# A hybrid encoder layer: weights split ahead of the feature tiles, and written orders from the decay terms to the merge

## The chip, the cores and the metric

The kernel runs on one core of a Trainium2 chip. The time is device microseconds of one execution; three executions of the kernel before give the median. A profiled execution has a trace of every instruction beside its time.

## What is computed

One layer, 256 tokens and 16 meta tokens (L = 272 positions) of 2048 features, float32:

```python
u = rmsnorm(h); proj = u @ W_in
# branch A: q, k = silu(conv3(...)); bidirectional mLSTM cell, 4 heads x 256
b = cumsum(log_sigmoid(f))
dmat = b[t] - b[s] + i[s];  m_t = max(...)
s = (q @ k.T) * exp(dmat - m_t)
hs = (s @ v) / maximum(abs(sum(s)), exp(-m_t)); head norm over 256
# branch B: differential attention, 8 heads, partial rotary on q and k
merged = sigmoid(g_A) * (A @ W_A) + sigmoid(g_B) * (B @ W_B)
h += merged @ W_out
h += ConvGLU(RMSNorm(h)); final RMSNorm
```

The forward and the backward cell are each computed in one piece, with the cumulative log decays on the rows of a matrix.

## The kernel before

All matrix products run with features or tokens on the 128 partitions. Every float32 operand is split into a high half (`hi`, a cast on ScalarE, line 157) and a low half (`lo`, a subtraction on VectorE, line 115), and `product` (line 172) issues three matmuls for each pair of operands: hi by hi, hi by lo, lo by hi. The weights come in pieces of 4 x 128 rows by 256 columns (512 KB), in the order of the list `pieces`. SyncE loads them (line 200) into six buffers, `prepare` splits them into four pairs of buffers, and `gemm` runs 24 matmuls on each piece. `gemm` is a generator: it yields after each piece, and `weave` steps a second generator once for each piece, so that the cell's work lies between pieces. What stands in the list `later` is issued at the next `flush`, after a piece.

The stages that matter here, in order:

- The opening: the tokens' features are turned (transposed on TensorE, line 349), scaled and split, two at a time, and the first block of query weights (pieces 0 to 3) is multiplied as the features come (`gq`, k = 0 to 15). Behind it are 32 small matmuls for the cell's gates (`gg`, the rows with 32 output columns), and the norm of the tokens, spread over the partitions by `spread_norm`. This whole stage stands inside `in_order()`: each engine runs it in the order in which it is written.
- The queries (pieces 4 to 15) and keys (16 to 31), with `conv_silu` behind each block: a multiplication by the norm that evacuates the accumulator, three taps of a convolution, Silu, split. Beside them `decay_terms` turns the gates into the decays. There are three accumulators `acc`, two per block, so that the second accumulator of a block needs the evacuation of the first of the block before.
- The values (32 to 47), transposed and centred by `turn`; beside them `heads1`: for each head the decays (a broadcast on GpSimd and exponentials), the scores, and the sums of the scores.
- The feature queries of branch B (`roped(dq)`, 48 to 63); beside them `heads2`: the reciprocal of the sums, `spread`, `merged`, `outputs`, `normed`.
- The feature keys (`roped(dk)`) and all that follows, to the end of the span.

Outside of `in_order()` a scheduler with a cost model decides, before the kernel is built, in which order each engine runs its instructions; data dependences bind it, the written order doesn't.

```python
def weave(front, back):
    for _ in front:
        next(back, None)
    run(back)
```

## Time and profile before

| | |
|---|---|
| three runs, us | 1567.14, 1569.33, 1570.07 (median 1569.33) |
| profiled execution, us | 1567.37 |
| its span, us | 1565.5 |
| instructions | 28927 |
| busy: TensorE, VectorE, ScalarE, GpSimd, us | 1542.6, 1028.6, 763.7, 81.0 |

The span runs from the first to the last instruction of the core; 1.9 us of the profiled execution's time lie outside it. An engine is busy while it runs an instruction; matmuls overlap one another, so TensorE's busy time doesn't say at which pace they run. In the rows, an operand's name is that of its tile, PE is TensorE, ACT ScalarE, DVE VectorE, POOL GpSimd, SP SyncE.

### The profile page before, as it was taken

What the parts mean: (1) busy time and instruction counts of PE and PEld (TensorE: products, weight loads), DVE (VectorE), ACT (ScalarE), POOL (GpSimd) and SP (SyncE); (2) the same over time, 40 slices, a digit from 0 to 9 for tenths busy, and PEclk for the clock granted to TensorE, in tenths of its full rate; (3) what the DMA queues carried; (4) which work ended last, traced back from release to release, by engine and by line L of the source; (5) the groups of instructions that cost most, each with busy time, mean ns of one, the idle gap of its engine ahead of it and who ended that gap; (6) DMA issues with size and microseconds to landing.
All of it is one profiled execution on the core that took longest, in us unless ns stands there. A gap on an engine that the chain in (4) does not pass through costs nothing.

```text
span 1565.5 us, 28927 instructions
## 1 busy us (share of the span) xinstructions
PE 1542.6 (99%) x11825; PEld 1491.2 (95%) x11825; DVE 1028.6 (66%) x1617; ACT 763.7 (49%) x1147; POOL 81.0 (5%) x120
## 2 busy tenths in 40 slices
PE   8899989999999999999999999999999999999997
PEld 8899989999999999999999999999888999999887
DVE  6786688758886545665666676666444676766554
ACT  5656445444655433554555444444333444545443
POOL 1130113100000000000110000000000000000000
PEclk9999999999999999999999999999999999999999
DMA  8365425654356655555555556555555556655552
GB/s 261 110 202 161 148 83 166 189 166 132 122 175 202 185 179 188 181 180 185 193 169 181 187 185 187 181 183 180 198 190 188 187 177 188 185 181 185 184 195 95
DMA packets 255386, 274.53 MB, mean 175 GB/s; under 512 B 11492, under 2 KB 233317, under 8 KB 255237
## 3 DMA queue, kind: packets, MB, share of 16 engines
q1 hardware_dynamic: 251378, 268.61, 54.1%
q10 hardware_dynamic: 3875, 4.07, 0.8%
q8 instruction: 93, 1.52, 0.4%
q14 instruction: 40, 0.33, 0.1%
HBM read 270.55 MB, written 2.10 MB: 174 GB/s over the span
## 4 chain that ended last, share of the span: by engine, by line
PE 95%; DVE 2%; ACT 1%; issue 1%; POOL 0%; DMA 0%; SPq 0%; DVEq 0%; POOLq 0%; ACTq 0%
PE acc L172 90%; PE two L172 2%; DVE lo L115 1%; PE two L846 1%; PE one L172 0%; PE one L858 0%; PE two L568 0%; POOL t L712 0%; ACT hi L157 0%; DMA r<-in_norm_g_dram 0%; PE two L977 0%; PE two L965 0%; DVE u L730 0%; DVE u L115 0%; POOL t L164 0%
## 5 line engine op out<-in xcount | busy, mean ns | idle before, releaser
L172 PE MATMUL acc<-u,hi 128*128 128x258 f32 (+1 forms) x6592 | 1201.8, 285 | 4.8 <-DVE r L161 4.8
L172 PEld LDWEIGHTS acc<-u,hi 128*128 128x128 f32 x6592 | 1019.0, 190 | 7.1 <-DVE r L161 5.1
L172 PE MATMUL acc<-u,lo 128*128 128x258 f32 (+1 forms) x3296 | 925.3, 284 | 0.8 <-DVE lo L115 0.8
L115 DVE TENSOR_TENSOR lo<-raw,hi 128x1024 fp32r<-128x1024 f32 (+1 forms) x500 | 616.8, 1234 | 422.1 <-ACT hi L157 420.4
L157 ACT CAST hi<-raw 128x1024 fp32r<-128x1024 f32 (+1 forms) x500 | 523.7, 1048 | 648.1 <-PE acc L172 501.5
L172 PEld LDWEIGHTS acc<-u,lo 128*128 128x128 f32 x3296 | 622.3, 190 | 1.9 <-DVE lo L115 1.2
L172 PE MATMUL acc<-hi,u 128*128 128x512 f32 (+1 forms) x704 | 209.6, 381 | 0.0
L172 PEld LDWEIGHTS acc<-hi,u 128*128 128x128 f32 x704 | 130.7, 190 | 26.3
L172 PE MATMUL acc<-lo,u 128*128 128x512 f32 (+1 forms) x352 | 134.9, 383 | 0.0
L172 PEld LDWEIGHTS acc<-lo,u 128*128 128x128 f32 x352 | 66.2, 188 | 13.6
L161 DVE TENSOR_TENSOR r<-acc,r 128x258 f32<-128x258 f32 x88 | 37.3, 424 | 12.2 <-PE acc L172 12.2
L115 DVE TENSOR_TENSOR u<-r,u 128x256 fp32r<-128x256 f32 (+2 forms) x93 | 37.7, 435 | 4.9 <-ACT u L157 4.4
L1025 ACT ACTIVATE r<-r,fcT 128x256 f32<-128x256 f32 x88 | 39.8, 500 | 0.0
L157 ACT CAST u<-r 128x256 fp32r<-128x256 f32 (+2 forms) x93 | 34.4, 404 | 9.7 <-DVE r L161 7.0
L1026 DVE SCALAR_TENSOR_TENSOR r<-r,fcT,r 128x256 f32<-128x256 f32 x88 | 38.5, 479 | 0.0
L1027 DVE SCALAR_TENSOR_TENSOR r<-r,fcT,r 128x255 f32<-128x255 f32 x88 | 38.4, 478 | 0.0
L151 ACT ACTIVATE r<-r 128x256 f32<-128x256 f32 (+2 forms) x77 | 29.5, 412 | 3.5 <-DVE r L459 3.1
L161 DVE TENSOR_TENSOR r<-r,r 128x256 f32<-128x256 f32 (+1 forms) x57 | 22.1, 420 | 0.1
L161 DVE TENSOR_TENSOR r<-acc,u 128x258 f32<-128x258 f32 x32 | 13.5, 422 | 12.9 <-PE acc L172 12.9
L164 DVE TENSOR_TENSOR u<-acc,u 128x512 f32<-128x512 f32 (+1 forms) x18 | 10.6, 626 | 13.9 <-PE acc L172 13.9
L161 DVE TENSOR_TENSOR r<-acc,rB 128x272 f32<-128x272 f32 (+1 forms) x38 | 16.1, 429 | 4.8 <-PE acc L172 4.7
L151 ACT ACTIVATE t<-two,sm 128x272 f32<-128x272 f32 x32 | 15.3, 482 | 5.5 <-DVE sm L802 5.5
(246 smaller groups left out, 754.6 us busy)
## 6 DMA issues: line engine op xcount, KB each, us to landing
raw<-in_w_up_dram SPq DMA_DIRECT2D x176, 512.0 KB, 3.9
raw<-in_w_in_dram SPq DMA_DIRECT2D x175, 512.0 KB, 3.5
raw<-in_w_down_dram SPq DMA_DIRECT2D x88, 512.0 KB, 3.7
raw<-in_w_out_dram SPq DMA_DIRECT2D x32, 512.0 KB, 3.3
raw<-in_w_branch_m_dram SPq DMA_DIRECT2D x16, 512.0 KB, 3.3
raw<-in_w_branch_d_dram SPq DMA_DIRECT2D x16, 512.0 KB, 3.2
t<-in_x_dram ACTq DMA_DIRECT2D x8, 256.0 KB, 3.4
xc<-in_x_dram SPq DMA_DIRECT2D x3, 512.0 KB, 6.3
```

What stands on the lines that cost most here:

```text
L115: V.tensor_tensor(out=out, in0=src, in1=hi.bitcast(F32), op=ALU.subtract)
L151: a = S.activation(out, in_, func, **kw)
L157: S.copy(hi, src)
L161: eng.tensor_tensor(out=o, in0=a, in1=b, op=ALU.mult)
L164: eng.tensor_tensor(out=o, in0=a, in1=b, op=ALU.add)
L172: PE.matmul(o, p, q, start=first and i == 0, stop=last and i == len(ops) - 1)
L846: PE.matmul(ps[:, i, 0:L], dq[h // 2][p][o:o + 64, h % 2, 2 + P * qt:2 + P * (qt + 1)], dk[h // 2][q][o:o + 64, h % 2, :], start=(p, q) == ...
L1025: S.activation(z, u[:, 2:NT], AF.Copy, scale=fcT[:, 1, f:f + 1])
L1026: V.scalar_tensor_tensor(out=z, in0=u[:, 1:NT - 1], scalar=fcT[:, 0, f:f + 1], in1=z, op0=ALU.mult, op1=ALU.add)
L1027: V.scalar_tensor_tensor(out=z[:, 0:SEQ - 1], in0=u[:, 3:NT], scalar=fcT[:, 2, f:f + 1], in1=z[:, 0:SEQ - 1], op0=ALU.mult, op1=ALU.add)
```

## The change

In the opening, piece i+1 is split ahead of the four groups of features that piece i meets, not after the second; the pieces 4 to 6 are prepared at k = 11, 13 and 15. From the decay terms to the feature keys, three `weave` calls move inside `in_order()`, so that the written order now holds there on every engine. And the written order changes: `conv_silu`'s evacuation only multiplies, and its taps, its Silu with the cast, and its low half each come one piece later (by `later`); `decay_terms` starts three pieces later; `decays` is divided into a broadcast and the exponentials, `scores` into the products, their weighing and their halves, `merged` into the merge and its halves, `outputs` and `normed` into the squares, the variance and the rest; the sums of a head are issued one head later, those of the last head in `heads2`, which is followed by the feature keys in the same `weave`. The absolute value of the sums becomes a maximum of the sums and their negatives on VectorE. `roped` rotates over three pieces. The number of matmuls stays the same.

```diff
         for k in range(16):
             if k % 4 == 0:
                 wq = weights(0)
+                if k < 12:
+                    prepare(k // 4 + 2)
             for ci in range(2):
                 product(gq[:, ci, :L], [([p[:, P * ci:P * (ci + 1)] for p in wq[k % 4]], [p[:, k % 2, :] for p in us[k // 2]])],
                         first=(k == 0), last=(k == 15))
             while turned < min(16, 2 * k + 4, k + 5):
                 turn(turned)
                 turned += 1
-            if k % 4 == 1:
-                prepare(k // 4 + 2)
             if k >= 5 and k % 2:
                 squares((k - 5) // 2)
             if k == 12:
 
                 split(wg[:, :, 0:16], wg[:, :, 16:32], graw)
-            if k in (12, 14):
-                prepare(k // 2)
+            if k in (11, 13, 15):
+                prepare((k - 1) // 2)
...
+        uc = []
+
+        def taps():
+            for ci, (u, c) in enumerate(uc):
+                S.activation(c, u, AF.Copy, scale=cw(1, f + ci))
+            for ci, (u, c) in enumerate(uc):
+                V.scalar_tensor_tensor(out=c[:, 1:nt], in0=u[:, 0:nt - 1], scalar=cw(0, f + ci), in1=c[:, 1:nt],
+                                       op0=ALU.mult, op1=ALU.add)
+                V.scalar_tensor_tensor(out=c[:, 0:nt - 1], in0=u[:, 1:nt], scalar=cw(2, f + ci), in1=c[:, 0:nt - 1],
+                                       op0=ALU.mult, op1=ALU.add)
+            later.append(silu)
+
+        def silu():
+            for ci, (_, c) in enumerate(uc):
+                activation(c, c, AF.Silu)
+                S.copy(hi[:, ci, :], c)
+            later.append(rest)
+
+        def rest():
+            for ci, (_, c) in enumerate(uc):
+                low(lo[:, ci, :], c, hi[:, ci, :])
+
         def evac(ci, a):
-            j = f + ci
-            u, c = r1(nt), r1(nt)
-            mul(u, a, r)
-            S.activation(c, u, AF.Copy, scale=cw(1, j))
-            V.scalar_tensor_tensor(out=c[:, 1:nt], in0=u[:, 0:nt - 1], scalar=cw(0, j), in1=c[:, 1:nt],
-                                   op0=ALU.mult, op1=ALU.add)
-            V.scalar_tensor_tensor(out=c[:, 0:nt - 1], in0=u[:, 1:nt], scalar=cw(2, j), in1=c[:, 0:nt - 1],
-                                   op0=ALU.mult, op1=ALU.add)
-            activation(c, c, AF.Silu)
-            split(hi[:, ci, :], lo[:, ci, :], c)
+            uc.append((r1(nt), r1(nt)))
+            mul(uc[ci][0], a, r)
+            if ci == 1:
+                later.append(taps)
...
     def decay_terms():
+        for _ in range(3):
+            yield
 
         pli, plf = two(), two()
         for d in range(2):
             PE.matmul(pli[:, d, :L], sel[0:32, d * P:(d + 1) * P], gsb[0:32], start=True, stop=True)
             PE.matmul(plf[:, d, :L], sel[0:32, (2 + d) * P:(3 + d) * P], gsb[0:32], start=True, stop=True)
         li, lf, e, y, w = (unit([2, L]) for _ in range(5))
+        yield
         S.copy(lf, plf[:, :, :L])
         S.copy(li, pli[:, :, :L])
...
+    with in_order():
+        weave(decay_terms(), chain(queries(), keys()))
...
+    last = []
+
     def heads1():
         activation(en, m[:, :, T0:L], AF.Exp, scale=-1.0)
-        decays(0)
+
+        broadcast(0)
+        broadcast(1)
         yield
         for h in range(4):
-            if h < 3:
-                decays(h + 1)
-            hl = scores(h)
-            yield
-            yield
-            yield
-            sums(h, hl)
-            yield
+            yield
+            decays(h)
+            yield
+            if h:
+                sums(h - 1, last[-1])
+            sc = scores(h)
+            yield
+            fs = weighed(h, sc)
+            if h < 2:
+                broadcast(h + 2)
+            yield
+            last.append(halved(fs))
 
     vm, gen = values(V0, True)
-    weave(heads1(), gen)
+    with in_order():
+        weave(heads1(), gen)
...
     def heads2():
+
+        yield
+        sums(3, last[3])
+        yield
         rec = unit([2, NT])
-        S.activation(rec, den[:, :, 0:NT], AF.Abs)
-        V.tensor_tensor(out=rec, in0=rec, in1=en, op=ALU.max)
+        V.scalar_tensor_tensor(out=rec, in0=den[:, :, 0:NT], scalar=-1.0, in1=en, op0=ALU.mult, op1=ALU.max)
+        V.tensor_tensor(out=rec, in0=den[:, :, 0:NT], in1=rec, op=ALU.max)
+        yield
         V.reciprocal(rec, rec)
+        yield
         rhl = pair(NT)
         split(*rhl, rec)
         yield
-        hl = merged(0, spread(0, rhl))
-        yield
+        rc = spread(0, rhl)
+        yield
+        FB = merged(0, rc)
+        yield
+        hl = halves(FB)
         yield
         for h in range(4):
+            num = outputs(h, hl)
+            yield
+            hi, lo = squared(num)
             if h < 3:
                 rc = spread(h + 1, rhl)
-            o = outputs(h, hl)
             yield
             if h < 3:
-                hl = merged(h + 1, rc)
-            normed(h, *o)
-            yield
-            yield
-            yield
+                FB = merged(h + 1, rc)
+            yield
+            if h < 3:
+                hl = halves(FB)
+            var, r = variance(hi, lo)
+            yield
+            normed(h, num, var, r)
...
-    weave(heads2(), roped(dq, DQ0, T0, NT))
-    run(roped(dk, DK0, 0, L))
+    with in_order():
+        weave(heads2(), chain(roped(dq, DQ0, T0, NT), roped(dk, DK0, 0, L)))
```

On TensorE, from the last matmul of the opening to the first of the gates. `acc` and `hi_396`, `lo_397` are accumulators and halves of piece 4 before, `two_171` is the gates' sum. Before:

```order
L172 MATMUL two_170<-u_166,lo_357 128x272
L172 MATMUL acc_559<-u_152,hi_396 128x258
L172 MATMUL acc_559<-u_153,hi_396 128x258
L172 MATMUL acc_560<-u_152,hi_396 128x258
L172 MATMUL acc_560<-u_153,hi_396 128x258
L172 MATMUL two_171<-u_152,u_172 32x272
```

In the change, the end of that stretch, where `hi_388` and `lo_389` are the halves of piece 4; ahead of it stand 18 more matmuls of piece 4:

```order
L172 MATMUL acc_532<-u_154,hi_388 128x258
L172 MATMUL acc_532<-u_155,hi_388 128x258
L172 MATMUL acc_532<-u_154,lo_389 128x258
L172 MATMUL acc_532<-u_154,hi_388 128x258
L172 MATMUL acc_532<-u_155,hi_388 128x258
L172 MATMUL two_171<-u_152,u_172 32x272
```

The gates stood behind 4 matmuls of piece 4, all of high halves; now they stand behind 23, with the low half among them.

On VectorE among the queries, up to the evacuation of an accumulator. Before, `r1_839` is that of the first accumulator of the third block of queries, behind the decay terms and their scans:

```order
L502 SCALAR_TENSOR_TENSOR u_548<-u_548,u_549 128x544
L505 SCALAR_TENSOR_TENSOR u_539<-u_548,u_547 128x272
L506 SCALAR_TENSOR_TENSOR u_539<-u_548,u_547 128x272
L512 MEMSET u_768 128x272
L516 SCALAR_TENSOR_TENSOR r1_771<-u_548,u_768 128x272
L525 SCALAR_TENSOR_TENSOR r1_805<-u_548,u_768 128x16
L161 TENSOR_TENSOR r1_839<-acc_703,rB_173 128x258
```

In the change, the evacuation of the second block's first accumulator (`r1_822`), behind three operations of the decay terms (`u_638`, `u_639`, `u_637`) and the low half of piece 13 (`lo_793`):

```order
L516 TENSOR_SCALAR u_638<-u_637 128x544
L517 TENSOR_SCALAR u_639<-u_638 128x544
L518 TENSOR_TENSOR u_637<-u_637,u_639 128x544
L115 TENSOR_TENSOR lo_793<-raw_686,hi_792 128x1024
L161 TENSOR_TENSOR r1_822<-acc_680,rB_173 128x258
L161 TENSOR_TENSOR r1_825<-acc_681,rB_173 128x258
L161 TENSOR_TENSOR u_637<-u_637,u_639 128x544
L115 TENSOR_TENSOR lo_834<-raw_722,hi_833 128x1024
```

On ScalarE in the change, the Abs, Exp, Ln and Exp of the decay terms and the casts of the pieces 12 to 14 (`hi_755`, `hi_792`, `hi_833`):

```order
L513 ACTIVATE u_637<-u_636 128x544
L142 ACT_TABLE_LOAD
L147 ACTIVATE u_637<-u_637 128x544
L157 CAST hi_755<-raw_644 128x1024
L151 ACTIVATE u_638<-u_638 128x544
L151 ACTIVATE u_639<-u_638 128x544
L157 CAST hi_792<-raw_686 128x1024
L157 CAST hi_833<-raw_722 128x1024
```

The scans no longer stand ahead of an evacuation here; a cast of weights now stands behind Ln and Exp, and an evacuation behind the low half that needs this cast.

On VectorE at the end of the values, in the change: the last weighing of scores (`FB_2022`), the reduction and the scaling of the last values, the low half of a piece (`lo_2485`), the low half of the last head's scores (`t2_2425`), and the sums' maximum and reciprocal (`u_2520`):

```order
L667 SCALAR_TENSOR_TENSOR FB_2022<-one_2358,FB_2022 16x2
L598 TENSOR_REDUCE sm3_2477<-two_2470 128x3
L599 TENSOR_SCALAR sm3_2477<-sm3_2477 128x3
L115 TENSOR_TENSOR lo_2485<-raw_2327,hi_2484 128x1024
L115 TENSOR_TENSOR t2_2425<-t2_2417,t2_2424 128x516
L609 SCALAR_TENSOR_TENSOR v0_1586<-two_2470,sm3_2477,v0_1585 16x256
L609 SCALAR_TENSOR_TENSOR u_2234<-two_2470,sm3_2477,u_2233 128x256 x2
L789 SCALAR_TENSOR_TENSOR u_2520<-two_1583,u_1584 128x516
L790 TENSOR_TENSOR u_2520<-two_1583,u_2520 128x516
L115 TENSOR_TENSOR lo_2524<-raw_2381,hi_2523 128x1024
L792 RECIPROCAL u_2520<-u_2520 128x516
```

Before, the low half of the scores stood ahead of the reduction, and the products that take it were spread among the matmuls of the feature queries; in the change TensorE has them behind 24 matmuls of the first piece of the feature queries and six transposes.

## Rows read from the trace of the kernel before

**Rows 1.** The page: the span, and the shares of the chain that ended last.

```profile
span 1565.5 us, 28927 instructions
...
PE 95%; DVE 2%; ACT 1%; issue 1%; POOL 0%; DMA 0%; SPq 0%; DVEq 0%; POOLq 0%; ACTq 0%
```

**Rows 2.** Waits of TensorE: us in total, times, longest.

```profile
PE acc L172 <- DVE r L161: 4.8, 1, 4.8
PE two L172 <- issue: 2.8, 1, 2.8
PE two L172 <- DVE lo L115: 1.8, 3, 0.7
...
PE two L172 <- DVE u L723: 1.0, 1, 1.0
PE acc L172 <- DVE lo L115: 0.8, 2, 0.5
PE one L172 <- POOL t L712: 0.5, 1, 0.5
PE two L172 <- DVE u L115: 0.3, 1, 0.3
```

**Rows 3.** Timeline of the opening: start, us, engine, line, operation, idle before.

```profile
22.63 9.70 SPq L200 DMA_DIRECT2D raw<-in_w_in_dram  x9
...
26.41 1.05 ACT L157 CAST hi<-raw 128x1024 fp32r<-128x1024 f32 x1 [1.35 <-DVE u L115]
...
27.49 1.23 DVE L115 TENSOR_TENSOR lo<-raw,hi 128x1024 fp32r<-128x1024 f32 x1 [1.10 <-ACT hi L157]
...
27.59 0.66 PE L172 MATMUL acc<-u,hi 128*128 128x258 f32 x4
...
28.09 4.14 PE L172 MATMUL two<-u 128*32 128x272 f32 x32
```

**Rows 4.** Busy time by window: PE, PEld, DVE, ACT, POOL, granted clock, DMA.

```profile
68.67:73.10 4.43, 4.43 (x20) 4.43 (x21) 4.43 (x15) 2.63 (x5) 0.00 (x0) 0.50 0.01 4
209.84:213.06 3.22, 3.22 (x17) 3.22 (x16) 3.22 (x12) 1.75 (x2) 0.86 (x1) 0.50 0.00 0
229.50:233.00 3.50, 3.50 (x30) 3.46 (x29) 3.50 (x9) 2.24 (x4) 2.47 (x2) 1.00 0.00 0
```

**Rows 5.** Timeline of the queries.

```profile
47.12 0.86 DVE L457 SCALAR_TENSOR_TENSOR r<-r,prmT,r 128x257 f32<-128x257 f32 x2
...
59.91 0.72 DVE L494 TENSOR_TENSOR u<-u 128x544 f32<-128x544 f32 x1
59.94 0.28 PE L172 MATMUL acc<-u,lo 128*128 128x258 f32 x1
...
60.30 0.28 PE L172 MATMUL acc<-u,lo 128*128 128x258 f32 x1
...
60.72 0.66 ACT L151 ACTIVATE u<-u 128x544 f32<-128x544 f32 x1 [1.02 <-DVE u L494]
...
61.40 1.28 ACT L147 ACT_TABLE_LOAD   x1
...
62.70 0.42 ACT L147 ACTIVATE r<-r 128x258 f32<-128x258 f32 x1
...
69.26 0.42 PE L172 MATMUL acc<-u,lo 128*128 128x258 f32 x1
...
69.91 0.42 PE L172 MATMUL acc<-u,lo 128*128 128x258 f32 x1
```

**Rows 6.** Busy time of the first eight pieces of the keys, columns as in Rows 4.

```profile
76.79:102.00 25.21, 24.43 (x195) 23.97 (x194) 22.82 (x33) 12.76 (x20) 15.96 (x27) 1.00 0.69 210
```

**Rows 7.** Timeline from the values to the first feature weights.

```profile
199.02 0.70 DVE L115 TENSOR_TENSOR t<-t,t 128x516 fp32r<-128x516 f32 x1 [1.44 <-ACT t L157]
...
199.63 0.95 DVE L573 TENSOR_REDUCE sm<-two 128x3 f32<-128x768 f32 x1
...
203.60 3.38 DVE L730 RECIPROCAL u<-u 128x516 f32<-128x516 f32 x1
```

More of the change, by code (lines that the diff above doesn't have):

```diff
@@ L326, in rsqrt, with newton @@
     def rsqrt(r, ss, n, work, bias=eps):
-        a, t = work
         activation(r, ss, AF.Ln, bias=bias, scale=1.0 / n)
         activation(r, r, AF.Exp, scale=-0.5)
+        newton(r, ss, n, work, bias)
+    def newton(r, ss, n, work, bias=eps):
+        a, t = work
         V.tensor_scalar(out=a, in0=ss, scalar1=1.0 / n, scalar2=bias, op0=ALU.mult, op1=ALU.add)
@@ L545, in queries @@
             yield from gemm(w_in, 16, Q0 + 256 * b, 256, us, T0, NT, conv_silu(qs, 2 * b, rQ, NT))
-    weave(decay_terms(), chain(queries(), keys()))
+    with in_order():
+        weave(decay_terms(), chain(queries(), keys()))
     def values(c0, centred):
@@ L569, in turn, with parts @@
                 pvs = pv[:, :, 0:384].rearrange("p c (s x) -> p s c x", s=3)
+                mu = sm(3)
                 if centred:
-                    mu = sm(3)
                     V.tensor_reduce(out=mu, in_=pvs, axis=AX.XY, op=ALU.add)
                     V.tensor_scalar(out=mu, in0=mu, scalar1=-1.0 / 256, scalar2=None, op0=ALU.mult)
+                later.append(lambda: parts(pvs, mu))
+            def parts(pvs, mu):
                 for s in range(3):
@@ L601, in hybrid_layer, with broadcast @@
     PARTS_W = [(F0c, 0, 0, 258), (F1c, 1, 2, 256), (F2c, 2, 130, 128)], [(B2c, 2, 0, 258), (B1c, 1, 0, 130), (B0c, 0, 0, 2)]
-    def decays(h):
+    def broadcast(h):
         FB = rbp.tile([P, WN], F32, tag="rb", name="FB")
@@ L617, in decays @@
         mask(FB[:, B2c + 130:B2c + 258], P, 0, 1)
+    def decays(h):
+        FB = W[h]
         for d, parts in enumerate(PARTS_W):
@@ L623, in scores @@
     def scores(h):
-        FB = W[h]
         ps, p0 = two(), one()
@@ L629, in scores, with weighed @@
             product(sc[s], [([t[:, c, s0:s0 + P] for t in ks[h]], [t[:, c, :] for t in qs[h]]) for c in range(2)])
+        return sc
+    def weighed(h, sc):
+        FB = W[h]
         for parts in PARTS_W:
@@ L643, in scores, with halved @@
         add(r[0:16, 0:2], r[0:16, 0:2], FB[0:16, B0c:B0c + 2], G)
+        return fs
+    def halved(fs):
         hi, lo = t2([2, NT], F32R), t2([2, NT], F32R)
@@ L698, in merged, with halves @@
         add(FB[:, B2c + 130:B2c + 258], FB[:, B2c + 130:B2c + 258], FB[:, F2c:F2c + P])
+        return FB
+    def halves(FB):
         hl = rbs.tile([P, 2, WN], F32R, tag="w", name="hl")
@@ L708, in outputs, with squared @@
                                        [t[:, 258 * s:258 * s + 258] for t in hl]) for s in range(3)])
+        return num
+    def squared(num):
         sq, hi, lo = t2([2, NT]), t2([2, NT], F32R), t2([2, NT], F32R)
@@ L712, in outputs, with variance @@
         G.tensor_tensor(out=lo, in0=sq, in1=hi.bitcast(F32), op=ALU.subtract)
-        return num, hi, lo
-    def normed(h, num, hi, lo):
+        return hi, lo
+    def variance(hi, lo):
         var = one()[:, 0:NT]
@@ L718, in normed @@
         r = r1()
-        rsqrt(r, var, 256, (r1(), r1()))
+        activation(r, var, AF.Ln, bias=eps, scale=1.0 / 256)
+        activation(r, r, AF.Exp, scale=-0.5)
+        return var, r
+    def normed(h, num, var, r):
+        newton(r, var, 256, (r1(), r1()))
         u = unit([2, NT])
@@ L757, in put, with swap, join @@
             dst.append((hi, lo))
+            sw = unit([2, nt])
+            table = lambda i: rope[:, i:i + 1, t0:t0 + nt].to_broadcast([P, 2, nt])
+            def swap():
+                V.stream_shuffle(sw, u, shuffle)
+                mul(sw, sw, table(1), G)
+                mul(u, u, table(0))
+                later.append(join)
+            def join():
+                add(u, u, sw)
+                S.copy(hi, u)
+                later.append(lambda: low(lo, u, hi))
             def evac(ci, a):
@@ L761, in evac @@
                 if ci == 1:
-                    table = lambda i: rope[:, i:i + 1, t0:t0 + nt].to_broadcast([P, 2, nt])
-                    sw = unit([2, nt])
-                    V.stream_shuffle(sw, u, shuffle)
-                    mul(sw, sw, table(1), G)
-                    mul(u, u, table(0))
-                    add(u, u, sw)
-                    split(hi, lo, u)
+                    later.append(swap)
             return evac
```

1 line of the change is left out of this document (added).

## The prediction

> **What bounds the kernel now.** I read the chain of the profiled execution first: 95% of the span is TensorE's own work [rows 1]. So a change of order on the other engines can only give back time in which TensorE waits, or runs slowly because it has waited. Next I read the waits of TensorE [rows 2], placed each on the timeline, and read the granted clock behind it [rows 4]. What can be recovered lies in three stretches:
>
> - Opening, until 27.6 us: three waits for the low halves of pieces 1 to 3, 1.8 us together.
> - Queries and start of the keys: one wait of 4.8 us (an accumulator is not free, because VectorE evacuates it late) and one of 0.5 us. Behind the long one the granted clock is 0.50, the lower level of 1.2 GHz, for 4.43 us [rows 4].
> - Values to the normalisation of the cell's heads: 2.8 and 0.3 us in which the products `spread` wait for the reciprocals, 1.0 us for a normalised head, 0.5 us for squares from GpSimd. Here too a stretch of 3.22 us at 0.50 follows the long wait [rows 4].
>
> The price of such a slow stretch comes from the pitch of the matmuls. From 59.94 to 60.30 three take 0.36 us, 0.12 each; from 69.26 to 69.91 three take 0.65, 0.215 each [rows 5]. A slow stretch therefore loses 1 - 0.12/0.215 = 0.44 of its length: 2.0 us in the queries, 1.4 us behind the values. The wait of 1.0 us had no such sequel: the window right behind it shows 1.00 [rows 4].
>
> So the change can win at most 1.8 + (4.8 + 0.5 + 2.0 = 7.3) + (2.8 + 0.3 + 1.0 + 0.5 + 1.4 = 6.0) = 15.1 us, 1% of the time, if it leaves no wait and makes none. The matmuls stay the same, and everything behind the feature keys keeps its order, so the whole question is what waits the new orders have. I followed the four queues of the changed program by hand with the durations of before.
>
> **Opening.** The split of piece i+1 now stands in front of the turns of its four tiles, and the three waits should go: the opening's matmuls would end at 27.6 - 1.8 = 25.8 us. But piece 4, the first of the next block, is not there yet. SyncE is still issuing small parameter loads and comes to it at 22.63; the cast on ScalarE runs from 26.41 to 27.46 and the low half on VectorE until 28.72 [rows 3]. The change moves none of that. Before, TensorE spent this time on the 32 gate matmuls (28.09, 4.14 us [rows 3]); in the new order these come behind 23 matmuls of piece 4. So TensorE idles from 25.8 to 27.46, runs two matmuls, and idles until 28.72. The remaining 22 matmuls of piece 4 (2.65 us) and the gates (4.0) end at 35.4. Before, the gates ended at 32.07 and 20 matmuls of the piece were left (2.4 us): 34.5. Result: the 1.8 us are won and lost again, and **0.9 us** more. An idle of 2.7 us out of 2.9 lies near the 2.8 + 0.3 that was followed by the lower clock and far from the 1.0 that was not, but two matmuls interrupt it; I charge half of 1.4, **0.7 us**. Bounds: 0 and 1.4.
>
> The Trainium skill (TensorE: Matmul & The Clock Gate, "Part 1: The HAM clock gate") says that an idle TensorE falls back to 1.2 GHz, at a phase that varies from run to run. The rows behind the long waits agree; by that page my half could be all or none in any execution.
>
> **Queries.** The 4.8 us went because VectorE had scheduled the evacuation of the old accumulator behind a long run of decay terms. In the new order the evacuation stands behind fewer, but TensorE's order is fixed too, with nothing to fill a gap. Four waits remain, counted from the end of the small products that spread the norm (time 0), with 0.35 to 0.42 us for an operation on 258 columns and about 0.7 for one on 544 [rows 5]:
>
> - The gate sums wait for the copy of the norm, three multiplications and a bias, 2.1 us, with 1.4 us of matmuls as cover: 0.7 us.
> - Piece 8: its cast stands behind two taps, the table load (1.28 us [rows 5]), two Silu and two casts, ready at 7.0 where TensorE arrives at 7.1; its low half takes 1.23 us more, and only two matmuls do without it: 0.9 us.
> - The next accumulator: its evacuation stands behind two small low halves and the low half of piece 9, and comes at 10.5; TensorE is there at 9.45: 1.1 us.
> - The accumulator after that. ScalarE ends the second Silu's cast at 14.8; then Abs 0.66, table load 1.28, Exp 0.66 (17.4), cast of piece 12 (18.45). VectorE makes the low half of it (19.7), two small low halves (20.4), and the decay terms' 0.44, 0.44 and 0.72 (21.9). ScalarE's Ln and Exp lie across these, to 22.6, and only then comes the cast of piece 13 (23.65), VectorE's low half of it (24.9), and behind that the evacuation (25.3). TensorE arrives at 22.05: 3.25 us. It is 4.8 us made shorter, not removed.
>
> Sum 5.95 us; and the wait of 3.25 lies between 2.8 + 0.3 and 4.8, which both brought the lower clock: 1.4 us by the nearer one. **7.35 against 7.3: nothing.** Bounds: without the lower clock -1.4; with 2.0 instead +0.6; each wait is the difference of two chains of ten to twenty operations, and I allow 2 us each way for their sum.
>
> In the keys' first half VectorE is busy for 22.82 of 25.21 us already [rows 6]; piece 16 would start at about the same time as before, so I charge no wait there. If VectorE falls behind, the evacuations of the keys wait with it (a rival below).
>
> **Values to the heads.** The chain behind the values is now spread over the steps of the feature queries. The reciprocal (3.38 us [rows 7]) gets four steps of 2.9 us as cover between the sums and `spread`, and the 2.8 + 0.3 us go; I find no wait for the 1.0 and the 0.5 either. But the last head's sums come after a single step of cover. Time 0 is the last matmul of the values: VectorE evacuates (0.6), weighs five blocks (2.7); TensorE has 24 matmuls (2.9) and six transposes (3.5) and then stands before the sums. VectorE goes on with the reduction (3.6 to 4.55, 0.95 [rows 7]), a small scaling (4.7), the low half of a weight piece (5.9) and only then the low half that the sums take (0.70 [rows 7]): 6.6. So a wait of **3.1 us**, as long as the 2.8 + 0.3 that it replaces, and by the same row 1.4 us of slow clock: 4.5 against 6.0, **-1.5 us**. Bounds: -2.9 without the clock; 0 if one of the two small waits stays.
>
> **Sum.** 0.9 + 0.7 + 0.05 - 1.5 = +0.15 us against the profiled execution (1567.37 us, of which 1.9 lie around the span). The median of the three runs is 1.96 above that execution, so the forecast is 1567.37 + 0.15 + 1.96 = 1569.5; I say **1569.3 us**, no change. A difference under 0.2% (3.1 us) is about what a measurement of this kernel can't tell from none.
>
> **Rivals.**
>
> - *The long wait in the queries does not appear.* It hangs on VectorE meeting the low half of piece 13 before the evacuation. If ScalarE's Exp and Ln run 3 us earlier against TensorE (every wait ahead of it shifts TensorE, not them), the 3.25 and its 1.4 fall away, and if the sums' wait also stays at the higher clock (-1.4) and the opening too (-0.7), the time is 1569.3 - 4.65 - 2.1 = 1562.6. For it: TensorE's own waits push it back against the chains, which are then less late. Against it: the chain on ScalarE and VectorE takes 10 us from the second Silu with nothing to shorten it. From 3.1 us on it counts as faster. Chance of faster 0.32.
> - *VectorE becomes the bound in the keys.* The place is 76.79 to 102, where 2.4 us of 25.2 are free on VectorE [rows 6]. In the fixed order an operation that waits (for GpSimd, for ScalarE) holds all behind it, weights' low halves included, so that idle can't be used by others. If VectorE waits 5 us in this stretch, 2.6 more than it has, TensorE loses these 2.6, and at the lower clock 1.4 more: 1569.3 + 4 = 1573.3. It decides from 5.5 us of such waits on. For it: the four waits above are of exactly this kind. Against it: half the decay terms' work was spread evenly over these steps. Chance 0.17.
> - *Every wait of about 1 us drops the clock.* Four such waits (0.7, 0.9, 1.1, and the opening's) at 1.4 each, 5.6 us: 1574.9. The 1.0 us wait with a clock of 1.00 behind it [rows 4] speaks against it. Chance 0.06. [...]
> - *The change does nothing it says*, because the waits merely move: that is my forecast. Chance 0.45.
>
> Faster 0.32, within 0.2% 0.45, slower 0.23. The range reaches from the first rival to the edge of the second and third: 1562 to 1574.5 us.
>
> **What would show it.** In the profile of the changed kernel: no waits of `two` for low halves before 25 us, but an idle of 2.5 to 3 us at 25.8 to 28.7; among TensorE's waits one for VectorE's multiplication (L161) of about 3 us near 64 and one of about 1; one near 205 of about 3 us that ends with VectorE's low half; a granted clock of 0.50 behind the two long ones. The forecast is wrong if one of the 3-us waits is missing (faster), or if waits of TensorE between 77 and 187 us, where there was one of 0.5, add up to over 3 us (slower).

## Result and profile after

The changed kernel takes 1582.59 us, the median of four runs (1578.87 to 1585.48), against 1569.24 of the kernel before on the same chip: ratio 1.0092, 95% interval 1.0079 to 1.0105. It is slower by 0.9%, 8 us past the upper end of the range. The profiled execution, the fastest of the four, took 1578.87 us; the rows below are from it. I read in the same order as before. First the page: the span, and the chain that ended last [rows 1].

```profile
span 1576.2 us, 28904 instructions
...
PE 93%; DVE 3%; ACT 1%; issue 1%; DMA 1%; SPq 0%; POOL 0%; ACTq 0%; DVEq 0%; POOLq 0%
```

The span is 10.7 us longer, and VectorE's share of the chain went from 2 to 3%. Next, what TensorE waited for (us in total, times, longest), to be held against [rows 2]:

```profile
PE two L172 <- DVE u L609: 5.3, 2, 2.7
PE acc L172 <- DVE r L161: 3.4, 2, 2.7
PE acc L172 <- DVE lo L115: 2.8, 4, 1.1
PE two L172 <- DVE t L115: 2.5, 2, 2.2
PE two L172 <- ACT t L157: 1.3, 2, 0.8
PE two L172 <- ACT hi L157: 1.2, 1, 1.2
```

The 4.8 us for an accumulator became 2.7, and the 2.8 for `spread` are gone. But the largest entry is new: 5.3 us for L609, a copy of centred values out of `two`. The rows of these waits on TensorE's timeline, from the opening to the feature keys:

```profile
12.02 0.36 PE L172 MATMUL two<-u,hi 128*128 128x272 f32 x1 [0.82 <-ACT u L354]
13.30 0.37 PE L172 MATMUL two<-u,hi 128*128 128x272 f32 x1 [0.92 <-DVE u L355]
...
29.11 0.39 PE L172 MATMUL acc<-u,lo 128*128 128x258 f32 x1 [0.76 <-DVE lo L115]
...
43.66 0.72 PE L504 MATMUL two<-r,t 32*128 32x272 f32 x2 [0.86 <-ACT r L491]
49.05 0.51 PE L172 MATMUL acc<-u,hi 128*128 128x258 f32 x2 [0.23 <-ACT hi L157]
50.31 0.39 PE L172 MATMUL acc<-u,lo 128*128 128x258 f32 x1 [0.75 <-DVE lo L115]
52.45 0.50 PE L172 MATMUL acc<-u,hi 128*128 128x258 f32 x2 [0.68 <-DVE r L161]
...
66.93 0.51 PE L172 MATMUL acc<-u,hi 128*128 128x258 f32 x2 [2.71 <-DVE r L161]
...
190.34 1.88 PE L172 MATMUL two<-u 128*128 128x258 f32 x12 [2.66 <-DVE u L609]
...
200.48 0.38 PE L172 MATMUL two<-t,selr 128*128 128x258 f32 x1 [0.42 <-ACT t L157]
...
203.06 0.63 PE L172 MATMUL two<-t,selr 128*128 128x258 f32 x3 [2.20 <-DVE t L115]
...
308.99 0.39 PE L172 MATMUL acc<-u,lo 128*128 128x272 f32 x1 [1.09 <-DVE lo L115]
```

Busy time by window, columns as in [rows 4]; the granted clock is the third figure from the end:

```profile
60.00:67.00 7.00, 4.29 (x37) 4.08 (x35) 5.12 (x9) 3.35 (x6) 0.00 (x0) 1.00 0.25 75
67.00:75.00 8.00, 8.00 (x67) 8.00 (x68) 7.27 (x11) 6.71 (x11) 0.00 (x0) 1.00 0.58 176
160.00:170.00 10.00, 6.47 (x48) 5.85 (x47) 3.47 (x7) 3.24 (x7) 1.68 (x4) 1.00 0.28 81
170.00:180.00 10.00, 9.70 (x67) 9.73 (x68) 5.92 (x12) 5.05 (x11) 3.64 (x7) 0.83 0.44 130
190.00:200.00 10.00, 9.66 (x66) 9.53 (x66) 6.01 (x12) 6.32 (x13) 1.69 (x4) 0.83 0.55 170
200.00:210.00 10.00, 7.39 (x59) 7.12 (x59) 8.74 (x11) 3.83 (x6) 0.00 (x0) 1.00 0.30 91
```

Behind the wait of 2.7 us at 66.9 and that of 2.2 us at 203 the clock stays at 1.00; two windows of the values' stage have 0.83, about a third of them at the lower level.

The matmuls are the same in number and nearly in order, so the start of the k-th one tells where the 10.7 us arose. The changed kernel is 1.4 us behind at the 200th (piece 4 and the gates), 0.8 ahead at the 1000th (early in the values), 5.8 behind at the 1800th (where the feature queries end), 7.6 at the 2400th (in the feature keys), 7.7 at the 6400th, 10.65 at the last. So: opening +1.4; queries, keys and the first values -2.2; **values to the heads +6.6**; feature keys +1.8; and about +3 in the feed-forward, where every engine's order is that of before. Of the 6.6, 4.5 are TensorE's waits (9.2 us between the 1000th and the 1800th matmul, against 4.6 before); most of the rest is the second of the two stretches at the lower clock, where before there was one.

**The values' stage, followed back.** TensorE, VectorE and ScalarE around the first long wait, from the timeline:

```profile
163.98 0.88 POOL L164 TENSOR_TENSOR t<-t,FB 16x258 f32<-16x258 f32 x2
164.90 0.62 ACT L157 CAST t<-t 128x516 fp32r<-128x516 f32 x1 [6.84 <-POOL t L164]
165.42 1.04 ACT L157 CAST hi<-raw 128x1024 fp32r<-128x1024 f32 x1
165.57 0.38 PE L172 MATMUL two<-t,selr 128*128 128x258 f32 x1 [0.84 <-ACT t L157]
166.37 0.46 ACT L608 ACTIVATE v<-two,sm 16x256 fp32r<-16x256 f32 x1
...
169.67 0.48 DVE L609 SCALAR_TENSOR_TENSOR u<-two,sm,u 128x256 fp32r<-128x256 f32 x1 [0.54 <-ACT u L608]
170.30 2.27 PE L172 MATMUL two<-u 128*128 128x258 f32 x12 [2.64 <-DVE u L609]
```

Read from the bottom: the scores' products of a head wait 2.64 us for a free `two`, which the copies of the values (L608, L609, in turns on both engines) still hold. These began only at 166.37, because in ScalarE's fixed order they stand behind the cast of the scores' sum `t`, and ScalarE had stood 6.84 us for GpSimd's additions (L164). So look at GpSimd:

```profile
142.22 1.89 POOL L164 TENSOR_TENSOR t<-t,FB 16x258 f32<-16x258 f32 x2
150.70 1.35 POOL L634 PARTITION_BROADCAST FB<-rows  x1 [6.58 <-PE two L172]
152.12 3.20 POOL L637 TENSOR_SCALAR_AFFINE_SELECT FB<-FB 16x2 f32<-16x2 f32 x6
163.18 0.83 POOL L164 TENSOR_TENSOR t<-FB 128x128 f32<-128x128 f32 x2 [7.86 <-issue]
163.98 0.88 POOL L164 TENSOR_TENSOR t<-t,FB 16x258 f32<-16x258 f32 x2
170.79 1.35 POOL L634 PARTITION_BROADCAST FB<-rows  x1 [5.93 <-issue]
172.22 2.29 POOL L637 TENSOR_SCALAR_AFFINE_SELECT FB<-FB 16x2 f32<-16x2 f32 x6
183.21 0.83 POOL L164 TENSOR_TENSOR t<-FB 128x128 f32<-128x128 f32 x2 [8.70 <-PE acc L172]
```

The additions of 163.18 had their inputs at 157.0 (VectorE's last weighing), yet GpSimd did nothing. Before each of these pauses its queue holds an instruction of its own, recorded twice at each place (count, then the first and the last start):

```profile
L634 POOLq MODIFY_POOL_CONFIG  x6: 1/1/11, 43.4 to 165.1; - x6
L164 POOLq MODIFY_POOL_CONFIG  x6: 1/1/1, 105.5 to 174.6; - x6
```

It stands ahead of a broadcast that follows another kind of operation (L634), and again ahead of the next addition (L164). From it to the next instruction pass 144.33 to 150.70, 155.35 to 163.18, 165.07 to 170.79 and 174.54 to 183.21: 6.4, 7.8, 5.7 and 8.7 us. The inputs of the two broadcasts were ready; those of the two additions came at 157.0 and 178.4, so the additions started 6.1 and 4.8 us behind them. The Trainium skill (GPSIMD Engine Reference, "2.1 Instruction dispatch") says that it loads code, and that the first call afterwards costs about 6 us that no instruction in the profile shows; the 5.93 and 6.58 us agree. In the kernel before all four broadcasts stood in a row, and the additions came 42 us later, so the two changes of code were hidden:

```profile
74.42 6.06 POOL L606 PARTITION_BROADCAST FB<-rows  x4 [30.45 <-PE acc L172]
80.32 12.44 POOL L609 TENSOR_SCALAR_AFFINE_SELECT FB<-FB 16x2 f32<-16x2 f32 x24
135.16 0.41 POOL L164 TENSOR_TENSOR t<-FB 128x128 f32<-128x128 f32 x1 [42.40 <-DVE FB L633]
```

The change moved `broadcast(2)` and `broadcast(3)` between the heads: four more changes of code, each in the path of a head.

### The profile page after: what moved, and what is told of

It reads as the page before. It is cut to its first block, busy times and chain, and to the rows that moved or that the text cites. A ratio compares the mean times of both kernels' runs of the same rounds, so it can differ in the third digit from the quotient of the medians.

```text
span 1576.2 us, 28904 instructions
## 1 busy us (share of the span) xinstructions
PE 1547.5 (98%) x11825; PEld 1494.4 (95%) x11825; DVE 1035.3 (66%) x1618; ACT 765.8 (49%) x1148; POOL 79.5 (5%) x120
## 4 chain that ended last, share of the span: by engine, by line
PE 93%; DVE 3%; ACT 1%; issue 1%; DMA 1%; SPq 0%; POOL 0%; ACTq 0%; DVEq 0%; POOLq 0%
PE acc L172 88%; PE two L172 2%; DVE lo L115 1%; DMA raw<-in_w_in_dram 1%; ACT hi L157 1%; PE two L927 1%; PE one L172 0%; PE one L939 0%; PE two L593 0%; DMA t<-in_lambda_k_dram 0%; PE two L1058 0%; PE two L1046 0%; DVE r L161 0%; POOL t L164 0%; ACT r L151 0%
## 5 line engine op out<-in xcount | busy, mean ns | idle before, releaser
L1106 ACT ACTIVATE r<-r,fcT 128x256 f32<-128x256 f32 x88 | 39.8, 500 | 0.0
L157 ACT CAST u<-r 128x256 fp32r<-128x256 f32 (+1 forms) x77 | 28.1, 404 | 9.4 <-DVE r L161 7.0
L843 ACT CAST u<-u 128x516 fp32r<-128x516 f32 (+1 forms) x8 | 5.1, 636 | 32.2 <-DVE u L164 32.2
L172 PE MATMUL two<-u 128*128 128x258 f32 (+1 forms) x96 | 14.1, 296 | 5.3 <-DVE u L609 5.3
```

The lines of the kernel that those rows point to most:

```text
L157: S.copy(hi, src)
L172: PE.matmul(o, p, q, start=first and i == 0, stop=last and i == len(ops) - 1)
L843: S.copy(hi, u)
L1106: S.activation(z, u[:, 2:NT], AF.Copy, scale=fcT[:, 1, f:f + 1])
```

## Experiments

"Before" in each is the kernel before on the same chip; a ratio is to it.

**1. All broadcasts ahead of the heads** (`e1`)

```diff
-        broadcast(0)
-        broadcast(1)
+        for h in range(4):
+            broadcast(h)
...
-            if h < 2:
-                broadcast(h + 2)
```

> The changed kernel, but all four broadcasts of the decay rows on GpSimd (each followed by its six masks) are issued at the start of the values' stage, not two there and two between the heads. Theory: in the profiled execution of the changed kernel GpSimd has a MODIFY_POOL_CONFIG on each side of the two later broadcasts, and 5.7 to 8.7 us pass from it to the next instruction; the additions of heads 1 and 2 are 5 to 6 us late by it, behind them the cast of the sums' scores on ScalarE, behind that the values' parts, and the scores' products on TensorE wait 2.64 and 2.66 us for these, each followed by a stretch at the lower clock (1.6 us). Expected: one such switch after the first stage and none between the heads, the two waits and the 0.84 + 0.35 of the sums gone, 9 to 10 us less than the changed kernel: a profiled execution near 1569, ratio to before 1.000 to 1.003. Rival: the scores wait because the values' parts were moved one piece later and share the PSUM buffer with the scores; then two waits of 2 us or more stay and the time is above 1576.

1572.48 us (1570.05 to 1574.31), ratio 1.0027 [1.0015, 1.0040]: 10 us of the 13 come back, or 8 of 12 by the changed kernel's second set of runs (`e8`, below). From the 1000th to the 1800th matmul this kernel takes 101.6 us, the changed one 111.0, the one before 104.4. So with this one move undone the rest of the stage's new order gains 2.8 us. The two windows that held 48 and 67 matmuls in the changed kernel are full, at a clock of 1.00:

```profile
160.00:170.00 10.00, 10.00 (x84) 10.00 (x83) 5.79 (x11) 6.67 (x14) 2.56 (x4) 1.00 0.50 145
170.00:180.00 10.00, 10.00 (x83) 10.00 (x82) 7.88 (x15) 4.83 (x8) 3.98 (x9) 1.00 0.47 121
```

**2. Values copied at once** (`e2`): the change of code stays, but the copies no longer stand behind the cast that waits for GpSimd.

```diff
-                later.append(lambda: parts(pvs, mu))
+                if centred:
+                    parts(pvs, mu)
+                else:
+                    later.append(lambda: parts(pvs, mu))
```

> The changed kernel, but the parts of the transposed values (centring and split, three on ScalarE and VectorE in turn) are issued right behind the transposes and the reduction, not one piece later. Theory of the switches on GpSimd: the switches stay, the additions of heads 1 and 2 stay 5 to 6 us late, the sums' waits stay (0.84 + 0.35 or more), but the parts no longer stand behind the late cast, so the two long waits of the scores go: 6 to 9 us less than the changed kernel, 1570 to 1573. Rival (the late parts alone are to blame): the same gain here, so this run tells the two apart only together with the one that moves the broadcasts: by the rival that one gains nothing.

1572.31 us, 1.0026 [1.0015, 1.0038]. The scores' waits for L609 are gone; the sums wait 1.17 + 0.34 and 2.28 + 0.35 us for the late additions. From the 1000th to the 1800th matmul it takes 106.1 us, 4.9 less than the changed kernel; another 2.2 us of its gain come from the feed-forward's pace (experiment 8) and have nothing to do with the copies. So the late addition costs twice: once itself, and again through what is queued behind its reader.

**3. The change of code without the work** (`e3`): experiment 1, with a broadcast of 64 columns, of no use, at the two old places.

> The kernel with all four broadcasts at the start, plus two small broadcasts of 64 columns into a tile that nobody reads, at the places where the changed kernel had the third and fourth. It computes the same. Theory of the switches on GpSimd: the size of the broadcast doesn't matter, the switch before and after it does; the additions of heads 1 and 2 are 4 to 6 us late again, the two long waits of the scores come back (2 to 3 us each) and the time is within 3 us of the changed kernel, near 1580. Rival: if the length of broadcast and masks made them late, the small broadcast costs nothing and the time is that of the kernel with four broadcasts at the start.

1574.24 us, 1.0040 [1.0025, 1.0055]: 1.8 us over experiment 1, which the two intervals don't separate, where I had expected most of the loss back. GpSimd's timeline shows the changes of code all the same:

```profile
147.90 1.89 POOL L164 TENSOR_TENSOR t<-t,FB 16x258 f32<-16x258 f32 x2
156.30 0.37 POOL L711 PARTITION_BROADCAST spare<-rows  x1 [6.51 <-issue]
163.38 0.82 POOL L164 TENSOR_TENSOR t<-FB 128x128 f32<-128x128 f32 x2 [6.72 <-ACT t L673]
```

Two changes and 0.37 us nearly fit between two heads; the additions start 0.7 and 1.4 us behind their inputs. The full broadcast and its masks (4.6 us, at 150.70 above) on top of that make 5 to 6. So the changes of code alone are not sufficient for the loss; what the broadcasts would cost there without a change of code, no run shows.

**4. The opening alone, and all but the opening.** `e4` is the kernel before with the opening's edit, `e5` the changed kernel with the old opening:

```diff
-                if k < 12:
-                    prepare(k // 4 + 2)
...
+            if k % 4 == 1:
+                prepare(k // 4 + 2)
...
```

> The kernel before with the change's opening alone (weights split ahead of each group of tiles, pieces 4 to 6 behind k = 11, 13, 15); all else, and the scheduler, as before. Theory: the three waits for low halves go (1.8 us), but the gates come behind piece 4's matmuls and TensorE idles 2 to 3 us for piece 4 (in the run with all broadcasts first: 2.59 + 0.76 us); 1 to 3 us slower than before, depending on the clock behind that idle. Rival: the opening by itself gains its 1.8 us and only the written orders behind it cost time; then 1.5 to 2 us faster than before.

> The changed kernel with the opening of before (splits behind k = 1, 5, 9, pieces 4 and 5 behind 12 and 14); all else as in the change. In the profiled executions the first matmul number 200 came 1.4 us later in the changed kernel. Theory: the new opening costs 1 to 1.5 us (waits of 0.8, 0.9 and 1.2 near the start in place of three of 0.6 at low halves, and the gates behind piece 4): this kernel is 1 to 1.5 us faster than the changed one, and the rest is the same. Rival: the new opening gains its 1.8 us, and this kernel is slower than the changed one by as much.

`e4`: 1570.57 us, 1.0013 [1.0004, 1.0022]. The three waits for low halves are gone, and 1.90 + 0.52 us for piece 4 stand at 28.16 and 29.42, close to the forecast idle of 2.7; it is 2.8 us behind at the 200th matmul. `e5`: 1578.71 us, 1.0065 [1.0050, 1.0080], with the waits of 2.66 and 2.56 us in the values. By these two pairs the opening's edit costs 2 to 4 us (more than the 1 to 1.5 expected of `e5`), not the rest. The profiled executions say the same: the 200th matmul comes at 35.4 to 39.8 us, 38.0 in the median, in the eleven of this document with the new opening and the gates behind piece 4, and at 34.6 to 35.4 in the five with the opening of before.

**5. The last long wait of the queries** (`e6`): experiment 1 with a `yield` ahead of Ln and Exp in `decay_terms`, so that the cast of piece 13 and the evacuation stand ahead of them.

```diff
         V.tensor_tensor(out=e, in0=e, in1=w, op=ALU.subtract)
+        yield
         activation(y, y, AF.Ln)
```

> All four broadcasts first, and one step more between the decay terms' subtraction on VectorE and the Ln and Exp on ScalarE (a yield); so the casts of the pieces 13 and 14 no longer stand behind Ln and Exp, which wait for VectorE. Theory of the prediction: the wait of 2.7 us of an accumulator for VectorE's multiplication in the queries goes, and the slow stretch behind it (1.7 us in the run with four broadcasts first): 2.7 to 4.4 us less than that run (1572.5), 1568 to 1570. Rival: VectorE is the bound there, and the wait comes back at another evacuation with 2 us or more; then the time is that of the run with the broadcasts first.

1567.73 us, 1.0000 [0.9991, 1.0009], 4.7 less than experiment 1, of which 0.6 come from the feed-forward's pace (experiment 8). The wait of 2.68 us is now

```profile
68.33 0.51 PE L172 MATMUL acc<-u,hi 128*128 128x258 f32 x2 [0.88 <-DVE r L161]
```

which confirms the chain that the prediction had for it.

**6. Gates ahead of piece 4** (`e7`): experiment 1, with piece 4 kept behind the 32 gate matmuls, the cover that they gave before.

```diff
+        gates_end = nc.cur_bb.bb.instructions[-1]
...
-    with in_order():
+    with in_order(gates_end):
         weave(decay_terms(), chain(queries(), keys()))
```

> All four broadcasts first, and the first matmul of piece 4 tied behind the last of the 32 gate matmuls (an order on TensorE alone). Theory of the prediction: the gates take 4 us in which piece 4's halves come, so the idle of 2.6 + 0.8 us ahead of piece 4 goes, the slow stretch behind it (1.3 us) too: 2 to 4.5 us less than the run with the broadcasts first (1572.5), 1568 to 1570.5. Rival: the gates wait for their own low half on VectorE or for something else, and the idle moves in front of them: no difference.

1572.81 us, 1.0024 [1.0014, 1.0034]: nothing gained. The wait moved to the gates, whose own low half is made behind piece 4's cast and low half, as the rival had it:

```profile
29.67 6.52 PE L172 MATMUL two<-u 128*32 128x272 f32 x29 [3.62 <-DVE u L115]
```

**7. All the repairs together** (`e10`): the old opening, experiments 1 and 5, and one `yield` more ahead of the last head's sums.

> The change with four edits: all four broadcasts first; Ln and Exp a step later; the opening of before; the last head's sums one step later (a second yield in front of them), so that VectorE and GpSimd have a piece more to make them. The rest of the change's orders stays. Theory: each wait is removed by itself and they add up: 1572.5 (broadcasts first) - 2.7 to 4.4 (Ln) - 1 to 3 (opening) - 2.6 to 4.2 (sums), 1561 to 1566, ratio to before 0.995 to 0.999: faster than both kernels. Rival: VectorE's 90% share in the keys and the heads binds, and waits removed at one place come back at the next: 1567 or more.

1562.69 us (1560.43 to 1564.03), 0.9965 [0.9953, 0.9978]: faster than both kernels, with no wait of TensorE over 1.7 us, and a granted clock of 1.00 from the first matmul to the last in its profiled execution. Of the 9.8 us against experiment 1, 3.2 come from the feed-forward's pace (experiment 8); of the 5.6 against the kernel before, 0.2. `e12` adds the new opening for pieces 2 and 3, an earlier load of piece 4, one more step for `decay_terms` and one ahead of `spread`:

> The kernel with the four edits (broadcasts first, Ln and Exp a step later, opening of before, sums a step later), and four more: pieces 2 and 3 split ahead of their tiles again (piece 1 not), piece 4's load issued ahead of the small parameter loads on SyncE, one step more in front of the first spread of the reciprocals, one more in front of the gate sums. Theory: two waits of 0.57 in the opening, 0.8 for piece 4, 1.7 in front of the spread go; 2 to 4 us less than with the four edits (1562.7): 1559 to 1561. Rival: the early load delays the tokens' and weights' loads ahead, or the waits come back behind the next operation: 1562 or more.

1563.06 us, 0.9966 [0.9953, 0.9978]: no better than `e10`, although it is 1.7 us ahead of it at the 6400th matmul. It loses 3.5 us in the feed-forward, which leads to the last question.

**8. The pace of the feed-forward.** Busy time of one window there, in the kernel before:

```profile
900.00:950.00 50.00, 50.00 (x421) 50.00 (x420) 35.40 (x56) 24.63 (x37) 0.00 (x0) 1.00 0.60 188
```

and in the changed kernel:

```profile
900.00:950.00 50.00, 50.00 (x418) 50.00 (x417) 34.13 (x50) 24.56 (x36) 0.00 (x0) 1.00 0.57 179
```

421 against 418 matmuls in 50 us, no wait, a full clock, the same order on every engine. A second run of both kernels (`e8`, `e9`) had 417 to 418 and 421 again: it belongs to the program.

> The changed kernel once more, unaltered. Two things vary between the executions seen so far: the granted clock behind the waits, and, between kernels, the pace of the matmuls of the up-projection far behind the change (418 matmuls in 50 us in the changed kernel, 421 in the one before, 3 us over that stage). Theory: the pace belongs to the program (where its tiles lie), so this execution shows 417 or 418 again; the opening and the queries may differ by up to 6 us by the clock; time 1578 to 1586. Rival: the pace belongs to the execution, and 420 or 421 can appear here.

> The kernel before once more, unaltered, one look. Theory as for the changed kernel: 420 or 421 matmuls in 50 us of the up-projection again, if the pace belongs to the program; the slow stretches behind 4.8 and 2.8 us of waiting in the same places. Rival: another pace.

`e8` took 1580.85 us, 1.0077 [1.0063, 1.0091], `e9` 1567.88. What differs is where the allocator puts the operands among the 48 equal slots of the pool `units` (2176 bytes per partition each). The first eight of the sixteen in their order of use, by slot; the matmuls in the window; and the time from the 6400th matmul to the last, us:

```
before, e4, e9                3 18  9 11 21 20 25 24   421         753.70
changed, e1, e3, e5, e7,
  e8, e11, e13               13 28  2 14 18  8 12 10   418         756.63
e6                           13 28  2 14 18  8 12 20   418         756.08
e2                           as changed, three others  420         754.46
e10                          12  4  2 14 18 13 27 10   421         753.48
e12, e14                      6 30  2 25 18 12 27  9   417         757.00
e15                          28 47 14 18  8 21 10  6   417         756.98
e16                          13 28  2 14 18  8 10  6   419         754.93
e17                           4 47 14 18 13 23 10 25   419         755.28
```

Executions of one layout agree within 0.01 us in the last column, on whatever chip they ran. TensorE waits nowhere in that stretch, in any of them.

`e11` exchanged the order in which the halves are requested (`lo, hi = pair(NT)`), but the allocator gave them the same slots, so it is only a further execution of that layout: 1579.98 us, 1.0088 [1.0067, 1.0109], pace 418.

> The changed kernel with one edit that changes no instruction's order: the tiles of the high and the low half of the feed-forward's input change places (lo, hi = pair in place of hi, lo = pair). The computation is the same. Theory of the places: the pitch of the up-projection's matmuls depends on where its operands lie, so it differs from 0.1203 us by at least 0.0002 here, in one or the other direction (the stage has some 5,600 of them: 1 us or more), and the opening up to the output projection is as in the changed kernel. Rival: the pitch doesn't depend on the places; 0.1203 again.

`e13` and `e14` move the whole pool behind the weights' pools (in the changed kernel and in `e12`), all operands by one distance:

> The changed kernel with every order kept and only the places of its small tiles in the state buffer moved (the pool of the heads' tiles is declared behind the pools of the raw and split weights, so the heads' tiles lie above the weights in place of below). Theory that places set the pace of the feed-forward stage: the pace leaves 417 to 418 matmuls per 50 us, up to 420 or 421, and the whole is 1 to 3 us shorter than the changed kernel, so some 8 to 11 us over the kernel before. Rival, that something else in the program sets it: 417 to 418 stay, and the whole stays at 10 to 12 us over the kernel before.

> The same move of the pool in the kernel of e12_more, which went at 417 matmuls per 50 us in the feed-forward stage and took 1563.06 us. If places set the pace: 420 or 421, and 1559 to 1561 us. If not: 417 to 418 and 1562 to 1564 us.

1581.98 us, 1.0081 [1.0066, 1.0096], and 1562.85, 0.9962 [0.9948, 0.9976]; the pace stays, as the rivals had it, and the stretch takes 756.63 and 757.00 us as without the move. The common place has no part in it, as far as this move shows. The last three change the slots relative to each other, by one tile that is requested ahead of the first (`e15`, `e17`) or the fourth pair (`e16`) of operands, `e15` and `e16` in the changed kernel, `e17` in `e10`. It adds one memset on GpSimd; the orders of the other engines are untouched.

```diff
+        if b == 0:
+            G.memset(unit([1]), 0.0)
         hi, lo = pair(NT)
         hs.append((hi, lo))
```

> The changed kernel with one tile more, a memset of one column on GpSimd ahead of the feed-forward's operands, so that those get other slots of the same pool; the rows of TensorE, VectorE, ScalarE and SyncE are the same. If the slots set the pace of the feed-forward stage it leaves 417 to 418 matmuls per 50 us, most likely upwards, and the time moves with it by 1 to 3 us. If slots have no part in it: 417 to 418, and 1579 to 1583 us.

> The same, with the extra tile ahead of the fourth pair of operands, so that the first six keep their slots and the others get new ones. If slots set the pace, some third value between 416 and 421 or one of the two known ones; if not, 417 to 418.

> The same extra tile in the kernel of e10_all, which went at 420 to 421. If slots set the pace it leaves 420 to 421, most likely downwards, by up to 4 matmuls per 50 us, and the time rises by up to 4 us from 1562.7. If not: 420 to 421 and 1562 to 1564 us.

`e15`: 1582.43 us, 1.0085 [1.0062, 1.0107]; `e16`: 1580.29, 1.0068 [1.0050, 1.0085]; `e17`: 1562.94, 0.9959 [0.9944, 0.9974]. The window in `e15`, `e16` and `e17`, one after the other:

```profile
900.00:950.00 50.00, 50.00 (x417) 50.00 (x416) 34.29 (x53) 24.65 (x36) 0.00 (x0) 1.00 0.59 180
```

```profile
900.00:950.00 50.00, 50.00 (x419) 50.00 (x418) 34.60 (x54) 24.44 (x36) 0.00 (x0) 1.00 0.62 183
```

```profile
900.00:950.00 50.00, 50.00 (x419) 50.00 (x418) 33.86 (x50) 23.59 (x33) 0.00 (x0) 1.00 0.62 187
```

`e15` and `e16` both carry the memset. `e15` takes 0.35 us more than the changed kernel from the 6400th matmul on (its expectation had the other direction as the likelier), `e16` 1.70 less; `e17` takes 1.80 more than `e10`. So the places of the pool's tiles relative to each other do set the pace. Which of them count, which places are good, and why, stays open; the extra tile also moves tiles that are taken later. The whole times of these pairs differ by less than their intervals.

## Why the prediction was wrong

**The step that failed** is in "Values to the heads". The prediction says that it followed "the four queues of the changed program", but there it followed VectorE's and TensorE's at the stage's end and said of the scores nothing at all. `broadcast(h + 2)` between two heads was a moved operation on a queue (GpSimd's) that was never followed, and its price, two changes of code of about 6 us around 4.6 us of work, was not in the sum. Measured: +6.6 us in this stage of the profiled execution, where -1.5 was forecast; undoing that one move gave 8 to 10 us back and left the stage at -2.8 (experiment 1), so the rest of its forecast stands. None of the rivals was this one. The nearest, an operation that waits for GpSimd and holds all behind it, was placed on VectorE in the keys, and there TensorE ran without a wait. The rows could have warned: GpSimd's 30.45 and 42.40 us of idle time around its broadcasts in the kernel before could hide any such price.

**Its own signs.** "Waits of TensorE between 77 and 187 us over 3 us (slower)" came: 3.9 us, of which 2.64 at 170.30. (The prediction's sum comes to 1569.5 us and is stated as 1569.3; nothing rests on that.)

**Opening: too low, and near in this execution by luck.** Forecast were +0.9 and 0.7 more for the clock; the profiled execution measured +1.4, but the median of the eleven executions of experiment 4 is 3.0 us behind that of the five with the old opening. In the profiled execution the waits for low halves of pieces went, and 0.82 and 0.92 us for the scaled features (L354, L355) came at 12 and 13 us: the splits of the next piece now stand ahead of them on ScalarE and VectorE. The matmuls so ended at 27.7 us, not at 25.8, and piece 4 cost 0.9 us instead of 2.7. Where those waits are smaller the forecast idle for piece 4 appears: 1.90 + 0.52 us in `e4`, 2.59 + 0.76 in `e1`. Why they differ from execution to execution stays open.

**Queries: right.** The four waits were forecast at 0.7, 0.9, 1.1 and 3.25 us and measured at 0.86, 0.23 + 0.75, 0.68 and 2.71: 5.2 against 5.95. Only the clock term was off: 1.4 us charged, and the clock stayed at 1.00, so this part gained 2.2 us instead of nothing. That term is not a property of the kernel: in `e1` the same wait of 2.68 us is followed by a window at 0.83. The Trainium skill (TensorE: Matmul & The Clock Gate, "Part 1: The HAM clock gate") calls the phase run-variable; the changed kernel's four runs agree, with mean clocks of 0.989 to 0.995 and spans of 1583.7 to 1576.2 us.

**Last head's sums:** 3.1 us forecast, 0.42 + 2.20 measured, again without the lower clock.

**"Everything behind the feature keys keeps its order"** was true and not enough: 3 us came from the slots. And within the feature keys 1.8 us were lost that the sum did not have; 1.09 of them are a wait for a late low half at 308.99. VectorE is busy for 11.79 of 12.00 us ahead of it, with the rotation, the last head's norm and the scalars of lambda among the low halves. That these make the low half late is argued from this row; no run removes them:

```profile
300.00:312.00 12.00, 10.74 (x84) 10.30 (x84) 11.79 (x24) 5.85 (x9) 1.90 (x1) 1.00 0.45 132
```

## What to carry

When an order is written by hand, follow every queue that a moved operation stands in, the idle one too; a pause that the profile puts down to "issue", or to an engine that was done long before, can be a price that the old order hid. On GpSimd keep broadcasts together and additions together, with idle time between the two kinds. An operation that reads a late result delays all that is queued behind it, so put such readers behind what others wait for. With all broadcasts first, Ln and Exp and the last sums a step later, and the opening of before, the written order is 0.35% faster than the scheduler's.

## Unexpected of the hardware

Each change between broadcasts and additions on GpSimd costs its queue a pause, not only the first of its kind, unless idle time covers it as in the kernel before. With inputs ready, a broadcast started 5.7 to 6.4 us behind the MODIFY_POOL_CONFIG (two cases in the changed kernel, two in `e3`). In the other direction an addition started 6.8 to 8.7 us behind it (two and two), but its inputs too came only 1.7 to 6.1 us behind it. And the matmul pace of a stage without waits, at a full clock, is 417 to 421 per 50 us by the places of the pool's tiles relative to each other: 753.5 to 757.0 us for the same matmuls, 3.5 us of this kernel.
